# One plain pair of feed-forward units instead of two, with VectorE's order of sums written out by hand

## The chip, the cores and the metric

The kernel runs on one core of a Trainium2 chip. The core has a matrix engine (TensorE, in the profile PE for matmuls and PEld for weight loads), a vector engine (VectorE, DVE), a scalar engine (ScalarE, ACT), GpSimd (POOL) and a queue engine that starts transfers (SyncE, SP). Each works through its own queue in order and waits on semaphores for the others. The metric is the device time of one execution in microseconds (us); smaller is better. The time before is the median of three runs.

## The reference

One layer of a hybrid decoder for two groups of requests at once, a prompt of 1024 tokens and 8 samples of 8 tokens, 1088 columns in all: windowed attention beside a convolution branch, both gated, then an output projection, a residual sum, and a feed-forward block with a short convolution. The change lies in the feed-forward block:

```python
up = rmsnorm(h, norm2_g) @ w_up                  # 1024 -> 2 x 2816
uc = dwconv_valid(up_ext, ffn_conv_w, ffn_conv_b)  # 3 taps along the tokens
gate, val = jnp.split(uc, 2, axis=-1)
y = h + (jax.nn.silu(gate) * val) @ w_down
```

All is float32. The 2816 gate columns are 22 units of 128, the value columns 22 more; gate unit f and value unit f make pair f.

## The kernel before

Activations lie transposed: 128 of the model's columns on the partitions, tokens along the free dimension. A float32 product is made of three matmuls in a faster type: each operand is split into a high part (a cast on ScalarE) and a low part (the difference, on VectorE), and `mm3` (L190) adds high x high, high x low and low x high. `split_ps` (L226) makes such a pair of parts and remembers the cast in `self.cast` and the difference in `self.low`. `w_load` and `w_split` load and split whole weight units.

The 1088 columns are four quarters of 272. `norm2` (L1292) makes the normalised rows of one quarter, splits them into `hh` and `hl`, and also writes them to memory (`d_n`). The up-projection, `ffn_up` (L1333), then runs over the 22 pairs in two ways.

- A **plain** pair (`plain`, L1432) multiplies two weight units with all four quarters over all eight blocks of 128 rows. Pairs 0 and 1 are plain (`PLAIN = 2`). In pair 0 the two units take turns by quarter; in pair 1 one unit follows the other.
- A **product** pair (`pair`, L1522) treats the two units, the two halves of the columns and the two halves of the rows as a 2 x 2 block product and makes it with seven half-size products instead of eight. The rows enter as blocks "11", "21" and "22", which are parts that the norm has made, and as four sums T1 to T4. The weights enter as four blocks and three sums, made on VectorE (`plan_pair`, L1488) and split into a ring of four tiles; `prep(n)` makes sure that n of them are traced. Seven products run in an order `seq`; each adds to bank A, E or C and is followed by an eviction into the pair's `st` rows: a copy on ScalarE where the row is new, a sum on VectorE where it is not. The next product on the same bank waits for that eviction.

The sums T1 to T4 serve all product pairs and are made once. `words(n)` (L1455) loads one of four groups of rows back from memory, four transfers on SP's queue, and `sums()` (L1467) makes of each group four differences on VectorE and splits each (16 differences, 16 casts, 16 low parts in all). Groups 0 and 1 need quarters 0 and 2, groups 2 and 3 need quarters 1 and 3.

After a pair, `finish` (L1402) makes the three-tap convolutions of its two units (one tap on ScalarE, two on VectorE, 1104 columns each), the gate and the store.

What sets the order: instructions are traced in the program's order, each with a priority that counts up; a planner puts them on each engine's queue by priority among those that it takes to be ready. `later(n)` shifts the priority of a block by n, and `issue_after(x)` puts what a block traces on x's engine behind x in that engine's queue. Tiles of one tag share `bufs` places and a new one waits for the release of an old one; in `ffn_up`'s pool, places lie in the order in which the tags are first used, over memory that the output projection has used before.

Of the kernel before, what the change touches and what calls it, by code (L numbers as in the profile page):

```python
# [9 lines left out]
ALU = mybir.AluOpType  # L10
AX = mybir.AxisListType

P = 128
# [23 lines left out]
AW = FW - 2  # L37
QW = T // 4
QUARTERS = [(c * QW, QW) for c in range(4)]
PLAIN = 2  # L40
PLAIN_LATER = 240
AHEAD = 3
UP_LATER = 100
# [11 lines left out]
HALF = T // 2  # L55
# [67 lines left out]
class Build:  # L123
# [1209 lines left out]
    def ffn_up(self, hh, hl, mp):  # L1333
        nc, tc, a, pool = self.nc, self.tc, self.a, self.pool
        f_es, t_es = ExitStack(), ExitStack()
        ft = pool(f_es, "ft")
# [9 lines left out]
        first = n_up + 2 * PLAIN  # L1346
# [10 lines left out]
        def slot(i):  # L1357
            if i < n_up:
                return old_slot(i)
            if i < first:  # L1360
                return (ft, ("wraw2", "wraw2")) if i == first - 1 else (self.wp, (i - first) % 2)
            if i == n_dn:
                return self.wp, 0
            if i == n_dn + 2:
                return self.wp, 1
            if i == n_dn + 3:
                return None, [self.t(self.ds, [P, T], f"e{x}", F32R)[:, :DM] for x in (7, 8)]
            if i in places:
                return None, [self.t(mp, [P, T], f"m{y}{places[i]}", F32R)[:, :DM] for y in "hl"]
            return self.wp, i % 2  # L1370
# [61 lines left out]
        def plain(f):  # L1432
            fs = (f, NF + f)
            ws = [self.weight(("up", x), 2 - n if f == 0 else 1) for n, x in enumerate(fs)] if f == 0 else [None] * 2
            both = [up_start(x) for x in fs]
            if f == 0:
                for c in range(4):
                    for w, b in zip(ws, both):
                        self.stream(None, xs, b[3], chunks=(c,), w=w, table=QUARTERS)
            else:  # L1440
                for x, b in zip(fs, both):
                    self.stream(("up", x), xs, b[3], chunks=range(4), table=QUARTERS)
            if f == 0:
                with self.later(-60):
                    sums()
            finish(f, both, PLAIN_LATER)

        def g_raws(n):
            for f in self.groups[n]:
# [4 lines left out]

        def words(n):  # L1455
            j, kk = groups[n]
            if n % 2:
                r = [self.t(ft, [P, FW], "acc", bufs=3)[:, :4 * QW].rearrange("p (x a b) -> p x a b", x=2, a=2)
                     for _ in range(2)]
                r = [t[:, x] for t in r for x in range(2)]  # L1460
            else:
                r = [self.t(ft, [P, 2, QW], "s", bufs=4) for _ in range(4)]
            for t, c, y in zip(r, (j, 2 + j, 2 + j, j), (0, 0, 1, 1)):
                nc.sync.dma_start(t, self.d_n[c, y][:, kk:kk + 2])
            loaded[n] = r

        def sums():  # L1467
            sub = lambda o, x, y: nc.vector.tensor_tensor(o, x, y, ALU.subtract)
            for n, (j, kk) in enumerate(groups):
                r11, r12, r22, r21 = loaded[n]  # L1470
                sub(r11, r12, r11)
                sub(r12, r22, r12)
                sub(r22, r22, r11)
                sub(r21, r21, r22)
                for x, r in enumerate((r11, r22, r12, r21)):
                    self.split_ps(th[x][j][:, kk:kk + 2], tl[x][j][:, kk:kk + 2], r)
                if n + 2 < len(groups):
                    words(n + 2)

        ring = {"n": 0, "tiles": []}  # L1480
        T1, T2, T3, T4 = range(4)
        B = {"11": lambda j: (hh[j][0], hl[j][0]), "21": lambda j: (hh[j][1], hl[j][1]),
# [3 lines left out]
        preps = []  # L1486

        def plan_pair(f):  # L1488
            i = n_up + 2 * f
            hw = DM // 2  # L1490
            live = {}

            def raws():
                while len(self.w_raw) < min(i + 4, len(self.order)):
                    self.w_load()
                ra, rb = self.w_raw[i:i + 2]
                live.update(a11=ra[:, :hw], a12=ra[:, hw:], a21=rb[:, :hw], a22=rb[:, hw:])
# [12 lines left out]

            preps.extend([
                split("a11"),
                split("a21", ("a11", "a11", "a21", ALU.subtract), ("a21", "a21", "a22", ALU.add)),
                split("a21", ("a21", "a22", "a11", ALU.subtract)),
                split("a21", ("a21", "a12", "a21", ALU.subtract)),
                split("a11"), split("a12"), split("a22")])

        def prep(n):
            while ring["n"] < min(n, len(preps)):
                preps[ring["n"]]()  # L1520

        def pair(f):  # L1522
            base = 7 * (f - PLAIN)
# [5 lines left out]
                ("A", "11", True, pg, 0, copy), ("E", T1, True, pv, 2, copy), ("A", T2, False, pg, 2, copy),  # L1529
                ("E", "22", False, pg, 2, plus), ("A", T3, False, pv, 2, plus), ("C", "21", True, pg, 0, plus),  # L1530
                ("A", T4, False, pv, 0, copy)]
            for n, (bank, b, fresh, parts, c, op) in enumerate(seq):
                prep(base + n + 1 + AHEAD)
                if f == NF - 1 and n == 4:
                    self.w_hl += [None] * (n_dn - len(self.w_hl))
                    self.w_stop = len(self.order)
                    for _ in self.groups[0]:
                        self.w_load()
                        self.w_split()
                wh, wl = ring["tiles"][base + n]  # L1540
                for j in range(2):
                    if fresh:
                        banks[bank, j] = self.bank("mm" if bank == "A" else "aux")
                    ps = banks[bank, j]
                    xh, xl = B[b](j)
                    for k in range(KT // 2):
                        ks = slice(k * P, (k + 1) * P)
                        self.mm3(ps[:, :QW], wh[:, ks], wl[:, ks], xh[:, k, :], xl[:, k, :],
                                 fresh and k == 0, k == KT // 2 - 1, not fresh)
                    for d, r in parts(c + j):  # L1550
                        op(d, r(ps))  # L1551
            finish(f, both)

        for f in range(PLAIN, NF):
            plan_pair(f)
        words(0)
        words(1)
        for f in range(PLAIN):
            plain(f)
        self.w_used = self.order.index(("dn", 0))  # L1560
# [360 lines left out]
```

## Time and profile before

| | |
|---|---|
| median of three runs | 1650.48 us (1650.45 to 1651.6) |
| the profiled execution | 1651.15 us, span 1649.3 us |
| TensorE matmuls busy | 1640.4 us, 99% of the span |
| VectorE busy | 1373.2 us, 83% |
| ScalarE busy | 864.8 us, 52% |
| granted TensorE clock | 1.00 |

The profile is of one execution. A row of the timeline has the start in us from the span's start, the duration, the engine, the line of the kernel, the operation, the tiles out<-in with their shape, how many instructions the row stands for, and in brackets how long the engine was idle before and who released it. A row of the windows has, for a stretch of time, the busy time of each engine with its count of instructions, then the granted clock, the share of the transfer engines and GB/s. A row of waits has the waiting engine and line, the one waited for, the total in us, how often, and the longest.

### The profile page before, as it was taken

What the parts mean: (1) busy time and instruction counts of PE and PEld (TensorE: products, weight loads), DVE (VectorE), ACT (ScalarE), POOL (GpSimd) and SP (SyncE); (2) the same over time, 40 slices, a digit from 0 to 9 for tenths busy, and PEclk for the clock granted to TensorE, in tenths of its full rate; (3) what the DMA queues carried; (4) which work ended last, traced back from release to release, by engine and by line L of the source; (5) the groups of instructions that cost most, each with busy time, mean ns of one, the idle gap of its engine ahead of it and who ended that gap; (6) DMA issues with size and microseconds to landing.
All of it is one profiled execution on the core that took longest, in us unless ns stands there. A gap on an engine that the chain in (4) does not pass through costs nothing. (4 is left out here: it accounts for less than half of the span.)

```text
span 1649.3 us, 30197 instructions
## 1 busy us (share of the span) xinstructions
PE 1640.4 (99%) x11606; PEld 1624.3 (98%) x11606; DVE 1373.2 (83%) x2474; ACT 864.8 (52%) x1795; POOL 257.3 (16%) x549
## 2 busy tenths in 40 slices
PE   9999999999999999999999999999999999999998
PEld 9999999999999999999999999999999999999997
DVE  7899979999979996788755887888888787989867
ACT  6524277774488845575533454444444454524222
POOL 0100112222011111121003421222222110000000
PEclk9999999999999999999999999999999999999999
DMA  6221222323121255648763532343334334766423
GB/s 210 84 63 51 63 73 69 100 92 99 55 62 41 90 191 188 197 149 217 200 217 107 188 107 79 107 115 113 114 114 117 92 100 135 262 158 165 109 61 109
DMA packets 104281, 200.47 MB, mean 122 GB/s; under 512 B 25928, under 2 KB 56648, under 8 KB 104120
## 3 DMA queue, kind: packets, MB, share of 16 engines
q1 hardware_dynamic: 80952, 130.49, 25.7%
q0 software_dynamic: 22752, 67.79, 14.0%
q8 instruction: 91, 1.49, 0.4%
q14 instruction: 54, 0.44, 0.1%
q10 hardware_dynamic: 432, 0.27, 0.1%
HBM read 136.44 MB, written 64.03 MB: 122 GB/s over the span
## 5 line engine op out<-in xcount | busy, mean ns | idle before, releaser
L192 PE MATMUL mm<-xh,whi 128*128 128x384 f32 (+1 forms) x904 | 301.5, 333 | 0.0
L194 PE MATMUL mm<-xh,wlo 128*128 128x384 f32 (+1 forms) x904 | 295.4, 327 | 0.0
L193 PE MATMUL mm<-xl,whi 128*128 128x384 f32 (+1 forms) x904 | 295.3, 327 | 0.1
L193 PEld LDWEIGHTS mm<-xl,whi 128*128 128x128 f32 x904 | 170.1, 188 | 1.2 <-DVE xl L279 0.4
L192 PEld LDWEIGHTS mm<-xh,whi 128*128 128x128 f32 x904 | 170.0, 188 | 0.7
L194 PEld LDWEIGHTS mm<-xh,wlo 128*128 128x128 f32 x904 | 169.7, 188 | 0.1
L1399 DVE SCALAR_TENSOR_TENSOR acc<-st,fc,acc 128x1104 f32<-128x1104 f32 x88 | 120.1, 1365 | 3.2 <-ACT acc L1397 1.9
L173 ACT CAST whi<-wraw 128x1024 fp32r<-128x1024 f32 (+1 forms) x65 | 62.7, 970 | 74.2 <-PE mm L193 53.1
L227 ACT CAST whi<-wraw 128x512 fp32r<-128x512 f32 x84 | 52.6, 626 | 76.8 <-PE aux L194 34.9
L227 ACT CAST wlo<-wraw 128x512 fp32r<-128x512 f32 x84 | 52.6, 626 | 74.9 <-PE aux L194 43.2
L522 DVE SCALAR_TENSOR_TENSOR bt<-u,consts,bt 128x513 f32<-128x513 f32 x120 | 89.7, 748 | 0.7
L522 DVE SCALAR_TENSOR_TENSOR c<-sm,hsum,c 128x512 f32<-128x512 f32 x120 | 89.6, 746 | 0.7
L192 PE MATMUL mm<-mh,whi 128*128 128x272 f32 (+4 forms) x296 | 88.1, 298 | 0.0
L194 PE MATMUL mm<-mh,wlo 128*128 128x272 f32 (+4 forms) x296 | 87.8, 297 | 0.0
L522 DVE SCALAR_TENSOR_TENSOR c<-u,consts,c 128x512 f32<-128x512 f32 x112 | 83.7, 747 | 0.5
L228 DVE TENSOR_TENSOR wlo<-wraw,wlo 128x512 fp32r<-128x512 f32 x84 | 60.9, 725 | 27.3 <-ACT wlo L227 25.5
L193 PE MATMUL mm<-ml,whi 128*128 128x272 f32 (+4 forms) x280 | 82.9, 296 | 0.0
L228 DVE TENSOR_TENSOR whi<-wraw,whi 128x512 fp32r<-128x512 f32 x84 | 57.9, 689 | 26.9 <-ACT whi L227 25.3
L174 DVE TENSOR_TENSOR wlo<-wraw,whi 128x1024 fp32r<-128x1024 f32 (+1 forms) x65 | 72.7, 1122 | 8.5 <-ACT whi L173 7.2
L1551 ACT COPY st<-mm 128x272 f32<-128x272 f32 (+2 forms) x140 | 46.9, 350 | 50.4 <-PE mm L194 50.4
L192 PE MATMUL aux<-mh,whi 128*128 128x272 f32 (+4 forms) x232 | 69.7, 300 | 0.0
L193 PE MATMUL mm<-tl,wlo 128*128 128x272 f32 x240 | 69.6, 290 | 0.0
(650 smaller groups left out, 5735.4 us busy)
## 6 DMA issues: line engine op xcount, KB each, us to landing
wraw<-wall SPq DMA_DIRECT2D x118, 512.0 KB, 4.4
bw<-d_b SPq DMA_DIRECT2D x42, 272.0 KB, 4.0
d_b<-gd POOLq DMA_DIRECT2D x36, 272.0 KB, 7.2
d_b<-acc POOLq DMA_DIRECT2D x24, 272.0 KB, 4.0
ar<-wdn SPq DMA_DIRECT2D x32, 192.0 KB, 3.4
d_g<-acc POOLq DMA_DIRECT2D x10, 544.0 KB, 4.2
ga<-d_ga SPq DMA_DIRECT2D x8, 544.0 KB, 4.5
ct<-d_c SPq DMA_DIRECT2D x8, 544.0 KB, 6.0
```

What stands on the lines that cost most here:

```text
L173: self.cast = self.nc.scalar.copy(h[:, z], r[:, z]).ins
L174: self.nc.vector.tensor_tensor(l[:, z], r[:, z], h[:, z].bitcast(F32), ALU.subtract)
L192: mm(ps, wh, xh, start=first, stop=False, skip_group_check=more)
L193: mm(ps, wh, xl, start=False, stop=False, skip_group_check=more)
L194: self.last_mm = mm(ps, wl, xh, start=False, stop=last, skip_group_check=more).ins
L227: self.cast = self.nc.scalar.copy(h, src).ins
L228: self.low = self.nc.vector.tensor_tensor(l, src, h.bitcast(F32), ALU.subtract).ins
L522: mac = lambda o, x, w: nc.vector.scalar_tensor_tensor(o, x, w, o, ALU.mult, ALU.add)
L1399: nc.vector.scalar_tensor_tensor(acc, st[:, k:k + AW], fw(f, k), acc, ALU.mult, ALU.add)
L1551: op(d, r(ps))
```

## The change

The constant `PLAIN` goes from 2 to 1, so pair 1 becomes a product pair. In that pair alone the product with block "21" comes second, right behind "11" (both need no sum), ahead of T1. The weight blocks are prepared in the same order.

`sums()` now chains all its steps with `issue_after`: each difference, each split and each weight part of pair 1 is put behind the step before it on VectorE's and on ScalarE's queue. Per group the order is difference, split (T1), difference, difference, split (T2), difference; the splits for T3 and T4 come at once in the first group and at the end for the other three. Between them stand the weight parts of pair 1: `prep(2)` after group 0, `prep(4)` after group 2, `prep(5)` after group 3, `prep(6)` and `prep(7)` among the last splits. The convolutions of plain pair 0 are put behind the chain's end, and so are pair 1's evictions, but for that of "11", which is put behind the first split's cast (`self.mark`).

The words of group 2 go to other buffers (two of tag `gd`, one of `acc`), so that they needn't wait for group 0's. The raw weights of pair 1 are loaded ahead of plain pair 0. The split weights of pair 0's second unit go into the two `wraw2` buffers, the first unit's into `whi1` and `wlo1`; two of the first down weights get other places.

```diff
-PLAIN = 2
+PLAIN = 1
@@ slot
-                return (ft, ("wraw2", "wraw2")) if i == first - 1 else (self.wp, (i - first) % 2)
+                return (ft, ("wraw2", "wraw2")) if i == first - 1 else (self.wp, 1)
             if i == n_dn:
-                return self.wp, 0
+                return self.wp, ("wlo1", "whi0")
             if i == n_dn + 2:
-                return self.wp, 1
+                return self.wp, ("wlo0", "whi1")
@@ plain
-            finish(f, both, PLAIN_LATER)
+            with tc.issue_after(self.chain[0]), tc.issue_after(self.chain[1]):
+                finish(f, both, PLAIN_LATER)
@@ words
-            if n % 2:
+            if n in (1, 2):
                 r = [self.t(ft, [P, FW], "acc", bufs=3)[:, :4 * QW].rearrange("p (x a b) -> p x a b", x=2, a=2)
-                     for _ in range(2)]
+                     for _ in range(3 - n)]
                 r = [t[:, x] for t in r for x in range(2)]
-            else:
+            if n == 2:
+                d = [self.t(ft, [P, HALF], "gd", bufs=2).rearrange("p (a b) -> p a b", a=2) for _ in range(2)]
+                r = [d[0], r[0], d[1], r[1]]
+            if n in (0, 3):
                 r = [self.t(ft, [P, 2, QW], "s", bufs=4) for _ in range(4)]
@@ sums
-            sub = lambda o, x, y: nc.vector.tensor_tensor(o, x, y, ALU.subtract)
-            for n, (j, kk) in enumerate(groups):
+            late = []
+
+            def step(go):
+                with ExitStack() as es:
+                    for x in self.chain:
+                        es.enter_context(tc.issue_after(x))
+                    self.chain = [go() or self.low, self.cast]
+
+            def sub(o, x, y):
+                step(lambda: nc.vector.tensor_tensor(o, x, y, ALU.subtract).ins)
+
+            def parts(n, x, r):
+                j, kk = groups[n]
+                step(lambda: self.split_ps(th[x][j][:, kk:kk + 2], tl[x][j][:, kk:kk + 2], r))
+
+            for n in range(len(groups)):
                 r11, r12, r22, r21 = loaded[n]
                 sub(r11, r12, r11)
+                parts(n, 0, r11)
+                self.mark = self.cast
                 sub(r12, r22, r12)
                 sub(r22, r22, r11)
+                parts(n, 1, r22)
                 sub(r21, r21, r22)
-                for x, r in enumerate((r11, r22, r12, r21)):
-                    self.split_ps(th[x][j][:, kk:kk + 2], tl[x][j][:, kk:kk + 2], r)
-                if n + 2 < len(groups):
-                    words(n + 2)
-
+                late += [(n, 2, r12), (n, 3, r21)]
+                if n == 0:
+                    words(2)
+                    while late:
+                        parts(*late.pop(0))
+                    words(3)
+                for x in ((1, 2), (), (3, 4), ())[n]:
+                    step(lambda: prep(x))
+            step(lambda: prep(5))
+            for part in sorted(late, key=lambda v: v[1]):
+                parts(*part)
+                if part[:2] == (3, 2):
+                    step(lambda: prep(6))
+            step(lambda: prep(7))
+
+        self.chain = []
@@ plan_pair
+            if f == PLAIN:
+                go.insert(1, go.pop(5))
+            preps.extend(go)
@@ pair
+            if f == PLAIN:
+                seq.insert(1, seq.pop(5))
             for n, (bank, b, fresh, parts, c, op) in enumerate(seq):
-                prep(base + n + 1 + AHEAD)
+                with ExitStack() as es:
+                    for x in self.chain if f == PLAIN else ():
+                        es.enter_context(tc.issue_after(x))
+                    prep(base + n + 1 + AHEAD)
...
-                    for d, r in parts(c + j):
-                        op(d, r(ps))
+                    with ExitStack() as es:
+                        for x in ([self.mark] if n == 0 else self.chain) if f == PLAIN else ():
+                            es.enter_context(tc.issue_after(x))
+                        for d, r in parts(c + j):
+                            op(d, r(ps))
@@ ffn_up
         words(0)
         words(1)
+        while len(self.w_raw) < first + 2:
+            self.w_load()
```

More of the change, by code (lines that the diff above doesn't have):

```diff
@@ L1509, in split @@
                 return go
-            preps.extend([
+            go = [
                 split("a11"),
@@ L1515, in plan_pair @@
                 split("a21", ("a21", "a12", "a21", ALU.subtract)),
-                split("a11"), split("a12"), split("a22")])
+                split("a11"), split("a12"), split("a22")]
+            if f == PLAIN:
+                go.insert(1, go.pop(5))
+            preps.extend(go)
         def prep(n):
```

## The prediction

> **What bounds the kernel now.** I read the page first, then who waited for whom on TensorE, then busy time by stage around the up-projection's start, then VectorE, ScalarE and the DMA queue in order of time there.
>
> ```profile
> span 1649.3 us, 30197 instructions
> PE 1640.4 (99%) x11606; PEld 1624.3 (98%) x11606; DVE 1373.2 (83%) x2474; ACT 864.8 (52%) x1795; POOL 257.3 (16%) x549
> ```
>
> ```profile
> PE mm L653 <- DVE warm L646: 1.1, 1, 1.1
> PE aux L420 <- ACT pth L227: 0.8, 1, 0.8
> ```
>
> TensorE is the bound of the whole; its waits (the two longest are shown) are under 3 us in all, none of them here. So a matmul removed is time saved and a TensorE wait added is time lost, each one for one. The question is who feeds TensorE where a stage is removed.
>
> ```profile
> core 0: us, PE busy (x) PEld busy (x) DVE busy (x) ACT busy (x) POOL busy (x), PEclk, DMA share, GB/s
> 921.50:946.20 24.70, 24.70 (x196) 24.62 (x195) 19.54 (x35) 12.05 (x27) 7.30 (x21) 1.00 0.62 202
> 946.20:958.30 12.10, 12.10 (x98) 12.10 (x97) 12.10 (x19) 7.49 (x14) 1.47 (x3) 1.00 0.45 157
> 958.30:970.40 12.10, 12.10 (x98) 12.10 (x97) 12.10 (x17) 8.61 (x14) 5.36 (x6) 1.00 0.01 1
> ```
>
> ```profile
> 921.55 0.29 PE L192 MATMUL mm<-mh,whi 128*128 128x272 f32 x1
> 958.32 0.29 PE L192 MATMUL mm<-mh,wraw 128*128 128x272 f32 x1
> 970.43 0.29 PE L192 MATMUL mm<-mh,whi 128*128 128x272 f32 x1
> ```
>
> Plain pair 0 starts at 921.55; the two units of plain pair 1 run from 946.2 (12.1 us before the change of weight tile at 958.32) to 970.43, where the first product pair starts. In just the 24.2 us of plain pair 1 VectorE is busy all the time: it makes there the operand sums that the products read. That is the cover which the change takes away.
>
> **The matmuls.** A plain unit is 4 quarters x 8 blocks x 3 = 96 matmuls in 970.43 - 958.32 = 12.11 us, 0.126 us each. A plain pair is 192, a product pair 7 x 2 x 4 x 3 = 168. One pair changes kind: 24 x 0.126 = 3.03 us saved, 0.18% of the time, the most that the change can give. The product pair now starts at 946.2 and would end at 967.4 where plain pair 1 ended at 970.43.
>
> **The chain on VectorE.** These rows give its prices.
>
> ```profile
> 933.36 0.45 DVE L228 TENSOR_TENSOR ml<-111l,mh 128x272 fp32r<-128x272 f32 x1 [0.45 <-ACT mh L227]
> 934.60 1.23 DVE L174 TENSOR_TENSOR wraw<-wraw,wraw 128x1024 fp32r<-128x1024 f32 x1 [0.79 <-ACT wraw L173]
> 935.74 1.48 DVE L1468 TENSOR_TENSOR s<-s,s 128x544 f32<-128x544 f32 x2
> 938.30 0.73 DVE L228 TENSOR_TENSOR tl<-s,th 128x544 fp32r<-128x544 f32 x1 [1.08 <-ACT th L227]
> ...
> 950.00 0.71 DVE L1468 TENSOR_TENSOR acc<-acc 128x544 f32<-128x544 f32 x1
> 950.63 0.71 DVE L1468 TENSOR_TENSOR s<-s,s 128x544 f32<-128x544 f32 x1
> ...
> 952.55 0.71 DVE L1468 TENSOR_TENSOR s<-s,s 128x544 f32<-128x544 f32 x1
> ...
> 960.23 0.69 DVE L228 TENSOR_TENSOR whi<-wraw,whi 128x512 fp32r<-128x512 f32 x1
> 960.84 1.36 DVE L1399 SCALAR_TENSOR_TENSOR acc<-st,fc,acc 128x1104 f32<-128x1104 f32 x1
> ...
> 962.11 0.72 DVE L228 TENSOR_TENSOR tl<-acc,th 128x544 fp32r<-128x544 f32 x1
> ```
>
> ```profile
> 937.62 1.20 ACT L227 CAST th<-s 128x544 fp32r<-128x544 f32 x2
> ...
> 953.29 0.65 ACT L227 CAST th<-s 128x544 fp32r<-128x544 f32 x1 [0.34 <-DVE s L1468]
> ...
> 958.39 0.62 ACT L227 CAST whi<-wraw 128x512 fp32r<-128x512 f32 x1 [0.64 <-PE mm L193]
> 958.92 0.64 ACT L227 CAST th<-acc 128x544 fp32r<-128x544 f32 x1
> ```
>
> A sum of 544 columns takes VectorE 0.635 us from start to start (950.00 to 950.63), a low part the same, a weight instruction of 512 columns 0.61 (960.23 to 960.84). A low part needs ScalarE's cast first: the sum of 952.55 ends at 953.26, the cast starts 0.03 later and takes 0.65, and a low part follows a cast by 0.03 (first cast of 937.62 over at 938.27, low part at 938.30). So a low part right behind the sum that it splits starts 0.71 + 0.03 + 0.65 + 0.03 = 1.42 us after that sum's start, not 0.635: VectorE stands for 0.79 us. In the weights it is 0.69 + 0.03 + 0.62 + 0.03 - 0.61 = 0.76.
>
> Before, the order was free, and other sums stood between most sums and their low parts. Now `step` pins VectorE and ScalarE each to one order: per group sum, part, sum, sum, part, sum. Both of these parts stand right behind their own sum (a group's other two follow later: the first group's at once, the rest at the chain's end). Nothing else may fill the hole, since the evictions and the convolutions of plain pair 0 are pinned behind the whole chain.
>
> Start: the last low part of the second norm is at 933.36, so VectorE is free at 933.7. Work on the second plain unit's weights (below) moves this by some 0.3: 934.0. The first group's words are no limit:
>
> ```profile
> 896.91 25.01 SPq L1464 DMA_DIRECT2D s<-d_n  x4
> DMA to landing us min/median/max: 2.8/3.3/4.9
> ```
>
> The four transfers are issued by 921.9 and land by 921.9 + 4.9 = 926.8. Yet the weight split of 934.60, which is traced later and so ranks lower, went ahead of the first sum at 935.74: the planner took the words to be ready only after the norm, and I expect no sum among the norm's instructions.
>
> Up to the sum for the weights of product "22" (`prep(5)`) the chain holds 26 instructions of 544 columns (8, 6, 6, 6) and 7 of 512 (two parts, then five for `prep(3)` and `prep(4)`): 26 x 0.635 + 7 x 0.61 = 20.8 us. Standing: 8 x 0.79 + 2 x 0.76 = 7.8. So the sum of `prep(5)` starts at 934.0 + 28.6 = 962.6. From there only ScalarE counts, for all its casts are pinned: 0.72 to the first one, then three weight casts (0.53 from start to start, 958.39 to 958.92) and six of 544 columns (0.55, from two in 1.20) up to the end of `prep(7)`'s: 0.72 + 3 x 0.53 + 6 x 0.55 = 5.6, so 968.2.
>
> The eviction of T1's product is a ScalarE copy pinned behind that last cast. The same bank takes product "22" next, so TensorE waits for it: one copy, here 0.39 + 0.03, to 968.6.
>
> ```profile
> 937.33 0.39 ACT L1390 COPY st<-mm 128x272 f32<-128x272 f32 x1 [2.48 <-PE mm L194]
> ```
>
> Then "22", T3 and T4 run without a wait, 3 x 24 x 0.126 = 9.1: the pair ends at 977.7. The low parts come in time (`prep(5)`'s at 962.6 + 1.37, then two weight parts and six others behind it, so that the last is over by 969.7; T4 starts at 974.7). Copies of plain pair 0 on ScalarE, one or two each 3 us until 949, can make a cast late: between 0 and 8 x 0.39 = 3.1 us; most fall into ScalarE's idle time, I take 0.5. End 978.2 against 970.43: +7.8.
>
> The wait is not one gap. T1 has its weights (`prep(3)`) only at about 955 instead of 952.3, its second half waits for the fourth group until 959.5, and T2 is done by 964; the last gap, to 968.6, is the longest, 4.6 us.
>
> **The second plain unit's weights** now go into two `wraw2` buffers which, by the order of first use in the pool, come to lie on the last output unit's weights.
>
> ```profile
> 921.42 0.29 PE L194 MATMUL mm<-t,t 128*128 128x272 f32 x1
> 933.50 1.07 ACT L173 CAST wraw<-wraw 128x1024 fp32r<-128x1024 f32 x1
> ```
>
> These are read until 921.71; cast 1.07 and low part 1.23 end at 924.0, and the second unit starts 24 matmuls and the norm's mean after 921.55, at 924.8. Cost on TensorE nothing by that order, some 0.3 on the norm. If the split ran where the split into `wraw2` ran before (933.5), plain pair 0 would be 10 us late, but the pair's end, set by the chain, would hardly move. That is why I charge 0 here.
>
> **What costs nothing.** The third and fourth groups' words: their rows are written with the norm's last parts (933.8 at the latest), two landings of 4.9 make 943.6, and the third group's first sum is at 947.5. The two early weight loads stand on SP's queue ahead of them, waiting for the split at 924.0, when no word is ready to be loaded. Plain pair 0's convolutions (4 x 1.27, then the gate) go from under plain pair 1 to behind 969.6; the next pair's first eviction needs their buffers at 981, five us after they can be done. POOL's store of plain pair 0's result goes with them; it is read only near the stage's end. The eviction of "11" stays early by `mark`. At the stage's end, the last pair's raw weights now share two buffers with the first down weights:
>
> ```profile
> 1382.50 0.69 DVE L228 TENSOR_TENSOR wlo<-wraw,wlo 128x512 fp32r<-128x512 f32 x1 [1.40 <-ACT wlo L227]
> ...
> 1384.51 1.05 ACT L173 CAST whi<-wraw 128x1024 fp32r<-128x1024 f32 x1 [2.05 <-PE aux L194]
> ```
>
> The pair's last weight part is over by 1383.2; a load as slow as the words' slowest (4.9), a cast and a part (2.3) end at 1390.4. At 1384.5 a product that frees the cast's buffer has ended, and three are still to run, 9.1 us, until 1393.6; only then are the down weights read. No cost.
>
> **Sum.** -3.03 for the matmuls, +10.8 of waits (978.2 - 967.4): +7.8. On the profiled execution, 1651.15 us (span 1649.3 and 1.85 around it), 1658.9; it is 0.67 above the median of 1650.48, which gives **1658.3**, 0.5% slower. About 0.2%, 3.3 us, is what a measurement of this kernel can tell from no change.
>
> **The clock.** Every window above has a granted clock of 1.00, beside TensorE pauses of 1.1 us at most. A pause of 4.6 us is new to this kernel.
>
> ```profile
> 1.05 5.49 PE L653 MATMUL mm<-mean 128*128 128x128 f32 x24 [1.05 <-DVE warm L646]
> ```
>
> The first 24 matmuls of the program, after idleness, took 0.23 us each for 128 columns, where 272 columns now take 0.126: TensorE can be slow after a pause. By the rows the price is between 0 and one product at half pace, 24 x 0.126 = 3.0; I take 0, as no pause in mid-kernel shows it. [...]
>
> **The rivals.**
> 1. The chain begins among the norm's instructions (words are there at 926.8, VectorE is nearly full until 933.7). Then the first two groups' holes, 4 x 0.79 = 3.2, are filled. From 926.8: the norm's rest (933.7 - 926.8 = 6.9) + 20.8 + 7.8 - 3.2 = 32.3, `prep(5)`'s sum at 959.1, the pair's end 3.5 earlier: +4.3, 1654.8. Against it: the order at 934.60.
> 2. The cover holds and the saving arrives: 1647.5. This is the other side. It needs "22" not to wait, so `prep(5)`'s sum by about 952.2, which is 10.4 us earlier than I put it; even with no hole at all the work of 20.8 from 933.7 ends at 954.5. It could be only if the order on VectorE were not serial as I read `step`.
> 3. The clock drops in the last gap: one product at half pace, +3.0, 1661.3.
> 4. Worse backlog: the convolutions, 4 x 1.27 + 1.2 + 0.2 = 6.5 us, stand ahead of the next pair's weights and TensorE waits for them too: up to 1664.8.
>
> **Chances.** The forecast 0.52 (its own range 1655.3 to 1660.9: the 0.5 between 0 and 3.1, the start up to 2.5 earlier); rival 1 0.15; rival 2 0.06; rival 3 0.19; rival 4 0.08. The range goes from 1652.0, below rival 1, to 1664.0. Slower by over 0.2% (above 1653.8): 0.52 + 0.19 + 0.08 and some 0.06 of rival 1, which may fill more holes than I count, 0.85; within 0.2%: the rest of rival 1 and most of rival 2, 0.13; faster 0.02, as the largest saving is itself below the bound.
>
> **What would show it.** In the profile after: 24 matmuls fewer; TensorE waits on VectorE's low parts or ScalarE's casts between 952 and 969, at T1, then at "22" behind the copy of T1's bank; VectorE's idle time before low parts 0.8 each, "<-ACT th"; a first sum at 934. I am wrong if the first sum starts by 930, if low parts don't wait for casts, or if T1's copy stands ahead of the last casts.

## The result, and the profile after

The changed kernel takes 1664.56 us (median of five runs, 1664.29 to 1666.61), the kernel before 1650.45 beside it: a ratio of 1.0088, with a 95% interval of 1.0073 to 1.0102, 14.1 us more. The prediction had 1658.3, 7.8 more, in a range that ended at 1664.0, 0.6 below the result. The direction was right and the size was not.

The page of the changed kernel, its first two lines:

```profile
span 1662.5 us, 30166 instructions
PE 1640.5 (99%) x11582; PEld 1623.3 (98%) x11582; DVE 1380.3 (83%) x2491; ACT 866.6 (52%) x1800; POOL 257.0 (15%) x549
```

There are 24 matmuls fewer, yet TensorE's busy time is what it was (1640.4): some of those that are left are slower. TensorE's longest waits there (waiting line, releaser, total, times, longest), and the stage in windows from the start of plain pair 0:

```profile
PE aux L192 <- ACT whi L227: 7.1, 1, 7.1
PE aux L192 <- ACT st L1594: 5.7, 1, 5.7
```

```profile
core 0: us, PE busy (x) PEld busy (x) DVE busy (x) ACT busy (x) POOL busy (x), PEclk, DMA share, GB/s
921.20:945.88 24.68, 24.68 (x197) 24.60 (x195) 16.30 (x31) 10.20 (x25) 7.02 (x21) 1.00 0.70 220
945.88:951.93 6.05, 6.05 (x50) 5.99 (x48) 4.59 (x8) 1.74 (x4) 0.38 (x2) 1.00 0.63 219
951.93:959.16 7.23, 0.16 (x2) 0.00 (x1) 5.01 (x9) 1.91 (x3) 0.00 (x0) 0.80 0.00 0
959.16:967.63 8.47, 8.44 (x48) 7.99 (x48) 6.29 (x10) 2.48 (x5) 0.00 (x0) 0.77 0.00 0
967.63:973.45 5.82, 0.17 (x3) 0.01 (x1) 5.08 (x9) 5.28 (x11) 0.00 (x0) 0.70 0.06 8
973.45:978.03 4.58, 4.58 (x24) 4.58 (x25) 4.55 (x8) 3.84 (x8) 0.00 (x0) 0.64 0.67 219
978.03:984.20 6.17, 6.17 (x51) 6.17 (x50) 6.12 (x12) 5.02 (x6) 4.54 (x6) 1.00 0.01 4
```

Plain pair 0, then "11" and "21", run as before. Then TensorE waits 7.23 us for T1's weights, takes 8.47 us for T1 and T2 (6.05 at full pace), waits 5.82 for the copies of T1's bank, and takes 4.58 for "22" (3.02 at full pace). The clock of 1.00 that every window before showed is 0.64 to 0.80 here. The pair ends at 984.20, 38.32 us after its start where 24.2 (the plain pair) minus 3.03 was ideal: 17.1 of waits and slow matmuls, less 3.03, is the 14.1.

VectorE and ScalarE in order of time there:

```profile
933.63 0.72 DVE L1481 TENSOR_TENSOR s<-s,s 128x544 f32<-128x544 f32 x1
937.96 0.73 DVE L228 TENSOR_TENSOR tl<-s,th 128x544 fp32r<-128x544 f32 x1 [3.62 <-ACT th L227]
938.61 1.48 DVE L1481 TENSOR_TENSOR s<-s,s 128x544 f32<-128x544 f32 x2
940.99 0.72 DVE L228 TENSOR_TENSOR tl<-s,th 128x544 fp32r<-128x544 f32 x1 [0.90 <-ACT th L227]
...
945.92 0.72 DVE L1481 TENSOR_TENSOR acc<-acc 128x544 f32<-128x544 f32 x1
947.36 0.72 DVE L228 TENSOR_TENSOR tl<-acc,th 128x544 fp32r<-128x544 f32 x1 [0.71 <-ACT th L227]
...
967.40 0.69 DVE L1536 TENSOR_TENSOR wraw<-wraw,wraw 128x512 f32<-128x512 f32 x1
968.82 0.69 DVE L228 TENSOR_TENSOR whi<-wraw,whi 128x512 fp32r<-128x512 f32 x1 [0.74 <-ACT whi L227]
```

```profile
937.00 0.39 ACT L1390 COPY st<-mm 128x272 f32<-128x272 f32 x1 [2.64 <-PE mm L194]
937.28 0.65 ACT L227 CAST th<-s 128x544 fp32r<-128x544 f32 x1
940.02 0.39 ACT L1390 COPY st<-mm 128x272 f32<-128x272 f32 x1 [2.09 <-PE mm L194]
940.31 1.20 ACT L227 CAST th<-s 128x544 fp32r<-128x544 f32 x2
943.05 0.45 ACT L1390 COPY st<-mm 128x208 f32<-128x208 f32 x2 [1.55 <-PE mm L194]
...
962.61 0.65 ACT L227 CAST th<-s 128x544 fp32r<-128x544 f32 x1 [1.40 <-DVE s L1481]
963.16 0.67 ACT L1594 COPY st<-mm 128x272 f32<-128x272 f32 x2
...
972.50 0.61 ACT L227 CAST whi<-wraw 128x512 fp32r<-128x512 f32 x1
973.01 0.72 ACT L1594 COPY st<-aux 128x272 f32<-128x272 f32 x3
```

The first sum runs at 933.63, as forecast. But its cast stands on ScalarE behind a copy of plain pair 0 that waits until 937.00 for TensorE, and so do the next casts: the second group begins at 945.92, not at the 941.9 that the prediction's prices give (934.0 + 8 x 0.635 + 2 x 0.79 + 2 x 0.61). From there on each low part that stands right behind its own sum has 0.7 us of idleness ahead of it.

Two things that the section on the change says, and the prediction with it, are not so in the trace. The eviction of "11" isn't behind the first split's cast: `self.mark` is set again in each group, and the rows of 962.61 and 963.16 show the copies behind the last group's. TensorE shows no wait there. And plain pair 0's weights don't go into new places: both units are split before `ffn_up` begins, during the output projection, into `whi` and `wlo`, and the trace has no other split of a whole unit up to 1000 us:

```profile
850.73 1.05 ACT L173 CAST whi<-wraw 128x1024 fp32r<-128x1024 f32 x1 [2.92 <-DMA wraw<-wall]
858.83 1.05 ACT L173 CAST whi<-wraw 128x1024 fp32r<-128x1024 f32 x1 [2.04 <-PE mm L193]
```

By the order in the program the first unit lies in `whi0` and `wlo0`, which are the places of pair 1's first two weight parts; e2 shows what that costs.

### The profile page after: what moved, and what is told of

It reads as the page before. It is cut to its first block, busy times and chain, and to the rows that moved or that the text cites. A ratio compares the mean times of both kernels' runs of the same rounds, so it can differ in the third digit from the quotient of the medians.

```text
span 1662.5 us, 30166 instructions
## 1 busy us (share of the span) xinstructions
PE 1640.5 (99%) x11582; PEld 1623.3 (98%) x11582; DVE 1380.3 (83%) x2491; ACT 866.6 (52%) x1800; POOL 257.0 (15%) x549
## 5 line engine op out<-in xcount | busy, mean ns | idle before, releaser
L228 DVE TENSOR_TENSOR whi<-wraw,whi 128x512 fp32r<-128x512 f32 x88 | 63.7, 724 | 30.1 <-ACT whi L227 28.5
L174 DVE TENSOR_TENSOR wlo<-wraw,whi 128x1024 fp32r<-128x1024 f32 (+1 forms) x62 | 69.0, 1118 | 7.1 <-ACT whi L173 6.8
L193 PE MATMUL mm<-tl,wlo 128*128 128x272 f32 x256 | 74.3, 290 | 0.0
L194 PE MATMUL mm<-th,wlo 128*128 128x272 f32 x256 | 74.0, 289 | 0.0
L192 PE MATMUL mm<-th,wlo 128*128 128x272 f32 x256 | 73.8, 288 | 0.0
L192 PE MATMUL mm<-mh,whi 128*128 128x272 f32 (+4 forms) x248 | 73.1, 295 | 0.0
L193 PE MATMUL mm<-tl,whi 128*128 128x272 f32 x248 | 71.9, 290 | 0.0
```

The costliest lines, as they stand in the source:

```text
L174: self.nc.vector.tensor_tensor(l[:, z], r[:, z], h[:, z].bitcast(F32), ALU.subtract)
L192: mm(ps, wh, xh, start=first, stop=False, skip_group_check=more)
L193: mm(ps, wh, xl, start=False, stop=False, skip_group_check=more)
L194: self.last_mm = mm(ps, wl, xh, start=False, stop=last, skip_group_check=more).ins
L228: self.low = self.nc.vector.tensor_tensor(l, src, h.bitcast(F32), ALU.subtract).ins
```

## The experiments

Three theories went in. A: the end of pair 1 is set by the pinned queues, and each of their delays has its own price: the holes on VectorE (its idle time between a sum and the low part that stands right behind it), copies ahead of casts on ScalarE, the evictions behind the chain's end. B: the slow clock after the pauses is what the prediction lacked. C: VectorE has too much work here once the plain pair is gone, in whatever order. The first four runs added D: VectorE's backlog, so that a wait taken from pair 1 comes back in pair 2.

Most runs write the queues of the stage out as lists, each instruction with `issue_after` behind the one ahead of it. In the lists, S is a difference, P a part (on ScalarE its cast, on VectorE its low part) of group a to d for T1 to T4, A a weight sum and W a weight part; c2 and c3 are the copies of plain pair 0's third and fourth quarter (g, v); 11, T1, ... are pair 1's evictions; a tap is one of the three terms of plain pair 0's convolutions, and conv one of those on VectorE. Written out in the changed kernel's order the lists give its stage: in e10, which only adds matmuls to it, T1 and "22" start 37.97 and 52.28 us after plain pair 0, in the changed kernel 37.96 and 52.24.

The table has each run's median, its distance from the kernel before beside it, and from the rows of its trace the start of T1, of "22", and the end of pair 2 (the first matmul of pair 3), counted from the start of plain pair 0. The medians are good to about 1 us; the last column shows smaller differences within the stage.

| run | us | minus before | T1 | "22" | pair 2 done |
|---|---|---|---|---|---|
| before | 1650.45 | 0 | | | 70.04 |
| changed | 1664.56 | +14.1 | 37.96 | 52.24 | 84.03 |
| e1 evictions placed | 1664.20 | +13.0 | 37.96 | 47.92 | 83.17 |
| e2 casts first | 1664.04 | +12.8 | 36.83 | 51.11 | 84.20 |
| e3 no holes, casts first | 1651.43 | +0.2 | 30.74 | 39.53 | 69.87 |
| e4 all three | 1651.62 | +0.4 | 30.73 | 36.84 | 70.44 |
| e5 unpinned | 1651.86 | +0.9 | 32.71 | 40.07 | 70.97 |
| e6 next weights first | 1648.17 | -2.8 | 30.73 | 36.78 | 67.85 |
| e7 kept busy | 1666.49 | +15.5 | 37.98 | 52.26 | 85.18 |
| e8 before, pinned | 1651.35 | +0.3 | | | 70.41 |
| e9 holes only | 1654.28 | +3.1 | 30.87 | 42.02 | 73.80 |
| e10 kept busy, pinned | 1664.21 | +13.0 | 37.97 | 52.28 | 82.62 |
| e11 e1 without taps | 1661.80 | +10.6 | 37.96 | 47.92 | 81.36 |
| e12 next casts first | 1647.78 | -3.4 | 30.73 | 36.78 | 67.11 |
| e13 start freed | 1661.23 | +10.0 | 34.00 | 48.28 | 80.48 |
| e14 holes back | 1656.12 | +4.9 | 34.00 | 43.69 | 75.51 |

### e1: the evictions placed

```diff
 ScalarE
-W5 Pb3 Pc3 Pd3 W6 Pb4 Pc4 Pd4 W7 T1a T1b T2a T2b
+W5 T1a T1b Pb3 Pc3 Pd3 W6 T2a T2b Pb4 Pc4 Pd4 W7
```

> Both queues of the stage are written out as one list, in the order that the changed kernel has, with one edit: the copies of T1's product stand on ScalarE right behind the cast of the weights for block 22, and T2's right behind the next weight cast, not behind the chain's last cast. Theory A (the pair's end is ScalarE's chain, with the evictions queued behind its end): by hand, with the durations of the changed kernel's trace, the 5.7 us wait before 22 shrinks to under 1 us, but 1.8 us come back before T4, so the pair ends 2.0 us earlier, and another 1.6 us if TensorE then isn't slow in 22: 1661.0 to 1662.6. Theory B (the slow clock after the pauses is what the prediction lacked): the pause of 7 us before T1 stays and so does its slow stretch; only 22 runs at full pace, 1.6 us less, 1663.0. Theory C (VectorE has too much work and its order doesn't matter): 1664.5.

"22" starts 4.3 us earlier, but pair 2 is done only 0.9 earlier. The pause before "22" is 1.3 us now and "22" runs at nearly full pace: the three groups of 24 matmuls that hold its own have means of 301, 288 and 288 ns, in the changed kernel 325, 315 and 312. The gain goes to new waits, at T4 for VectorE's sum (1.2 us) and in pair 2 for its weights (1.3, 0.9 and 0.2). Theory A had a wait before T4 in its sum; no theory had those in pair 2.

### e2: the casts first

```diff
 ScalarE
-c2g Pa1 c2v Pa2 Pa3 c3g Pa4 W1 W2 c3v Pb1 Pb2
+Pa1 c2g Pa2 Pa3 Pa4 c2v W1 W2 Pb1 c3g Pb2 c3v
```

> One edit to the changed kernel's order: the copies of plain pair 0's third and fourth quarter stand on ScalarE behind the casts that are ready before them (the first behind the chain's first cast, not ahead of it). VectorE's order and the pinned evictions stay. Theory A (a copy that waits for TensorE holds up the cast behind it, and with it VectorE): first low part at 935.1 and not 938.0, the group 3.6 us earlier, the chain's end too; pair 1 ends 3.6 us earlier, 1661.0, and if the shorter wait before T1 (3.5 us) brings no slow stretch, up to 1.6 us less, 1659.4. Theory B (slow clock): both pauses are still there (3.5 and 4.7 us), so 1664. Theory C (amount of VectorE's work): 1664.5.

T1 is 1.1 us earlier, not 3.6. The copies hold nothing up any more, but the first weight part does. ScalarE and VectorE of this run:

```profile
942.60 0.62 ACT L1508 CAST whi<-wraw 128x512 fp32r<-128x512 f32 x1 [2.51 <-PE mm L202]
```

```profile
943.25 0.69 DVE L1495 TENSOR_TENSOR whi<-wraw,whi 128x512 fp32r<-128x512 f32 x1 [2.81 <-ACT whi L1508]
```

Its place is free only when the matmuls of the first plain unit's last quarter end. The profile before has the same wait, at plain pair 1's first unit:

```profile
943.26 1.05 ACT L173 CAST whi<-wraw 128x1024 fp32r<-128x1024 f32 x1 [1.42 <-PE mm L193]
```

Behind the copies this wait was covered; without them it is the next in line. The clock then took the rest of the gain: it was 0.5 for 10.24 us from 967.97 here, and "22" took 5.6 us.

### e3 and e4: no holes, and all three

```diff
 VectorE (e3 and e4; e4 also has 21a 21b ahead of Sd4)
-Sa1 Pa1 Sa2 Sa3 Pa2 Sa4 Pa3 Pa4 W1 W2 Sb1 Pb1 Sb2 Sb3 Pb2 Sb4 Sc1 Pc1 Sc2 Sc3 Pc2 Sc4 A3 W3 A4 W4 Sd1 Pd1 Sd2 Sd3 Pd2 Sd4 A5 W5
+Sa1 Sb1 Sa2 Pa1 Sb2 Pb1 Sa3 Sb3 Sa4 Pa2 Pb2 Pa3 Pa4 W1 W2 Sc1 Sc2 Sb4 Pc1 A3 Sc3 W3 A4 Sd1 Pc2 W4 Sd2 Pd1 Sd3 A5 Sc4 Pd2 W5 Sd4
 ScalarE (e4; e3 has the copies of T1 and T2 behind W7)
+... Pd3 T1a W6 T1b Pb4 Pc4 Pd4 T2a W7 T2b
```

> As the run with the casts first, and VectorE's order is changed too: another group's sum or weight sum stands between a sum and the low part made of it, so that VectorE never waits for a cast; the evictions stay behind the chain's last cast. Theory A: the last weight part of the four that 22 needs moves from 968 to 954.5, the last cast to 958, and TensorE waits 0.4 us in the pair, 967.8 at its end (before: 970.4): 1647.8, below both kernels. Theory B has nothing to slow the clock when the waits are gone, the same 1648. Theory C: the 33 instructions that 22 waits for are still 20.8 us of VectorE after 933.7, with 2 us of low parts and copies behind: no better than 1655.

> All three edits in one order: casts first, no holes, and the copies of T1 and T2 and the sums of block 21 at the place where they are ready. Theory A: no wait of TensorE in the pair, the full 3.03 us of the matmuls saved: 1647.4; as the run before it has 0.4 us of waits left, the two differ by 0.4 us at most. If the difference is larger, placing the evictions is worth more than my schedule by hand has it. Theory C: no better than 1655.

Both come out at the kernel before's time (ratios 1.0001, intervals 0.9992 to 1.0010 and 0.9993 to 1.0010), 13 us under the changed kernel: theory C is out, and the clock is 1.00 in e4's windows below and in e3's in the last section. But neither is below before, which A had. TensorE's waits of e3 and of e4:

```profile
PE aux L201 <- ACT st L1516: 2.6, 1, 2.6
```

```profile
PE aux L201 <- ACT whi L236: 1.3, 2, 0.9
PE aux L203 <- DVE whi L237: 0.6, 1, 0.6
PE mm L201 <- ACT wlo L236: 0.2, 1, 0.2
```

e3 waits at "22" for its pinned copy, e4 doesn't, and waits 2.1 us in pair 2 instead, at its T1, T2 and "22", for weights. Two windows of e4, pair 1 and pair 2, show why:

```profile
945.79:967.27 21.48, 21.48 (x171) 21.27 (x170) 21.26 (x38) 15.12 (x30) 2.34 (x6) 1.00 0.25 81
967.27:991.55 24.28, 22.17 (x171) 21.29 (x169) 23.17 (x35) 13.11 (x24) 11.23 (x14) 1.00 0.25 85
```

VectorE is busy nearly all the time (21.26 of 21.48, then 23.17 of 24.28): the sums, then plain pair 0's convolutions, then pair 2's weights. That is theory D.

### e5: the changed kernel without its pins

```diff
 step() in sums()
-    for x in self.chain:
-        es.enter_context(tc.issue_after(x))
-    self.chain = [go() or self.low, self.cast]
+    go()
 and the same for the pins of evictions, weights and finish()
```

> The changed kernel without any of its pins: the sums, splits, weight parts, evictions and convolutions stand as the planner puts them, and all else (one plain pair, 11 and 21 first, the buffers) stays. Theory A (the pinned order is what costs): the planner puts other work between sums and their low parts and the evictions where their products end; with its queues laid out by hand TensorE waits 2.8 us before T1 and 1.0 in T2, so the pair ends at 971.3 where the changed kernel's ends at 984.6: 1651.3, up to 1652.6 with a convolution's tap on ScalarE between casts. Theory D, from the runs so far (VectorE's work until pair 2 is a bound; a wait taken from pair 1 comes back in pair 2): about 1651 as well, with waits in pair 2. Theory C (one plain pair less costs 14 us in any order): 1664.

1651.86, 0.9 above before, which is no difference that the runs can tell (ratio 1.0004, 0.9995 to 1.0013). One plain pair less costs nearly nothing in the planner's own order, where a wait of 1.8 us before T1 and one slow stretch behind it (3.41 us at a clock of 0.50) take back what the matmuls save; the pinned order costs the rest.

### e6 and e12: the next pair's weights ahead of the convolutions

```diff
 VectorE
+... Pa4 Sc1 Sc2 W1 W2 ... W7 22a 22b W8 A9 T3a T3b W9 A10 conv W10 conv conv conv
 ScalarE, e6 and e12
+... Pa4 c2v Pc1 W1 W2 ... T2a W7 T2b W8 tap tap W9 (e6: T4a T4b W10, e12: W10 T4a T4b)
```

> The run with all three edits, and the work behind the chain written out too: the first three weight blocks of pair 2 stand ahead of the convolutions of plain pair 0, ScalarE's Silu behind these casts; and in the chain the first two sums of the third group stand ahead of pair 1's first weight parts, which wait for plain pair 0's matmuls until 943.2. Theory A with a backlog behind it (pair 2's four waits of 2.7 us, for weights that stand behind convolutions, are all that is left): no wait in pair 1 nor in pair 2, 2.7 us under the run with all three, that is 2.5 below before. Theory D (VectorE simply has too much work here): the wait turns up in pair 2's block 22 or T3, or in its evictions, whose st buffers are free only after the convolutions, and the time stays within 0.5 us of before.

> The fastest run so far with one edit: the cast of pair 2's third weight block stands ahead of the two copies of T4, which wait for TensorE until 969.5 and kept VectorE idle for 1.75 us. Theory D (VectorE's free time is what counts in pair 2): the 0.85 us that TensorE still waits in pair 2 shrink by 0.5 or more, 0.4 to 0.8 below that run, that is 3.0 to 3.6 us below before. Rival: its last waits come from evictions on ScalarE, and it is the same within 0.3 us.

e6 is 2.8 us under before (0.9979, 0.9970 to 0.9988), e12 3.4 (0.9982, 0.9973 to 0.9991): both are faster than both kernels, and than the one before by about the 3.03 of the matmuls. The step from e6 to e12 is within the medians' spread, but in the last column it is 0.74, as expected. e12's windows of plain pair 0, pair 1 and pair 2:

```profile
921.74:946.44 24.70, 24.70 (x197) 24.62 (x196) 21.45 (x40) 12.08 (x28) 9.38 (x21) 1.00 0.79 245
946.44:967.50 21.06, 21.06 (x170) 21.06 (x169) 20.84 (x38) 13.98 (x28) 2.35 (x6) 1.00 0.26 85
967.50:988.85 21.35, 21.35 (x170) 21.29 (x170) 20.18 (x29) 12.65 (x23) 5.81 (x11) 1.00 0.21 77
```

TensorE has no wait, VectorE is busy 62.47 of the 67.11 us (21.45 + 20.84 + 20.18). Theory D's backlog is real, but it fits.

### e7 and e10: TensorE kept busy

```diff
+for _ in range(n):   # e7: 50 before T1, 40 before "22"; e10: 55, 24 before T1's second half, 36, each pinned in TensorE's queue
+    nc.tensor.matmul(idle[:, :QW], self.identr, hh[0][0][:, 0, :], start=True, stop=True)
```

> The changed kernel with added work: 50 matmuls of 272 columns into an unused bank before T1 (6.3 us at 0.126, in its wait of 7.1) and 40 before 22 (5.0 us, in the wait of 5.7), so that TensorE isn't idle in its two waits. Their results are not used. Theory B (the slow clock after a pause): no slow stretch; T1 and T2 take 6.1 us and not 8.5, which the chain takes back as a longer wait before 22, and 22 takes 3.0 and not 4.6: 1.55 us less, 1663.0. Rival: the slow stretches cost nothing, because ScalarE's chain sets the end whatever TensorE does: 1664.5 or, as the added matmuls stand in TensorE's queue, up to 0.5 more.

> The changed kernel's two orders written out, TensorE's too, with added matmuls of 272 columns pinned into its three waits: 55 before T1, 24 before T1's second half, 36 before 22 (6.9, 3.0 and 4.5 us); their results are not used. The run before with added matmuls left a pause of 3.5 us before 22, and 22 ran wholly in a slow stretch. Theory B, the clock's share: no stretch below full clock in this stage, 22 takes 3.0 us and not the changed kernel's 4.6, and starts at the same place, since ScalarE's chain sets it: 1.5 us below the changed kernel, 1663.0, and 3.5 below the run before. Rival: the time of the changed kernel, as something else than the pause slows 22.

In e7 the planner moved some of the added matmuls up, which left a pause of 3.5 us before "22", and "22" took 5.6 us at a clock of 0.50: 1.4 worse than the changed kernel. T1 and T2 ran at full pace (clock 1.00 from 953.4 to 969.1), and "22" started where it had (52.26 us, in the changed kernel 52.24). So the slow clock in T1 and T2 costs nothing here; the chain sets the start of "22". In e10, "22" has a window at full clock:

```profile
974.78:977.92 3.14, 3.14 (x25) 3.14 (x25) 3.01 (x7) 3.14 (x8) 0.00 (x0) 1.00 0.64 222
```

Pair 2 is done 1.41 us earlier than in the changed kernel. That is the clock's share of the 14.1.

### e8: the kernel before with its sums pinned

```diff
 before.py, sums(): each sub() and split_ps() in a step()
+with issue_after(last low or sum), issue_after(last cast): ...
```

> The kernel before, with both plain pairs, and of the change only the order of the sums: each difference and split pinned behind the step before, in the changed kernel's order (difference, split, difference, difference, split, difference; the splits for T3 and T4 at once in the first two groups, at the end in the others). Weights, evictions and convolutions are free. Theory A (the plain pair is a cover of 24.2 us): the chain, 32 x 0.635 + 8 x 0.79 = 26.6 us of VectorE from 934, with two taps and five weight instructions among it, ends about 966 to 970, T1 reads from 973.4: no change, within 0.5 us of before. If the pinned order were bad in itself, TensorE would wait at T1 or T2 of the first product pair, and the time be 2 to 6 us longer.

No change (ratio 1.0004, 0.9995 to 1.0013). With the plain pair as a cover of 24 us the same pinned order of the sums is free.

### e9: the holes alone

```diff
 VectorE as in e3; ScalarE keeps the copies ahead of the casts, evictions behind W7
+c2g Pa1 c2v Pb1 Pa2 Pb2 Pa3 c3g Pa4 W1 W2 c3v Pc1 W3 Pc2 W4 Pd1 ...
```

> The changed kernel with one edit, VectorE's order without holes (the order of the run with no holes); plain pair 0's copies stand ahead of the chain's first casts as in the changed kernel, and the evictions behind the chain's last cast. Theory A (the holes are the largest price): by hand the pair ends 9.8 us earlier, with no slow stretch 1.6 more: 1653.2; what VectorE's backlog takes back in pair 2 comes on top, 0 to 2 us. Rival (the copies and the place of the first weight block set the chain's start, the holes come second): the start of the second group stays where it is, about 945 against 945.9, and the gain is under 5 us, 1660 or more.

+3.1 and a last column 10.2 below the changed kernel's: one edit takes back three quarters of the loss, which puts the rival out. Part of it may be that VectorE, with other sums to do, isn't held up by the late casts; this run doesn't part the two. A pause of 3.1 us before "22" is left, and "22" still takes 4.58.

### e11: e1 without plain pair 0's taps on VectorE

```diff
-for k in (1, 2):
+for k in (1, 2) if f % NF else ():
```

> The run with the evictions placed, with plain pair 0's four convolution taps on VectorE left out (4 x 1.28 us; pair 0's result is not the reference's). Theory D (the 4.3 us that placing the evictions gained at block 22 went to VectorE's backlog in pair 2: its weights stand behind the convolutions): pair 2's waits at T1, T2 and 22, 2.9 us, are gone and the time is 2.5 to 3 us below the run with the taps, 1661. Rival (the waits in pair 2 come from ScalarE or from the evictions' buffers): no more than 1 us below it.

Pair 2 is done 1.8 us earlier than in e1, and the time is 2.3 under e1's distance from before: a little under the 2.5 that was expected at least. Pair 2 keeps waits of 0.4 and 0.3 us for weights, which this run doesn't explain.

### e13 and e14: the start freed, and the holes put back

```diff
 VectorE, both runs
-W1 W2 Sb1 Pb1 Sb2
+Sb1 Pb1 Sb2 W1 W2
 ScalarE, both runs; e13 is e2 with this edit, e14 is e12 with the changed kernel's order of sums and parts
-c2v W1 W2 Pb1 c3g Pb2 c3v
+c2v Pb1 W1 W2 c3g Pb2 c3v
```

> The run with the casts first, and pair 1's first two weight parts stand behind the first part and the second sum of the second group, so that their wait for plain pair 0's matmuls (until 943.1) holds up nothing. Holes and evictions stay as in the changed kernel. If the copies and the place of the first weight block together are what made the chain late: the second group's first sum starts at 940.7 and not 944.5 or 945.9, T1 at 20 us less than the changed kernel's end of the chain by hand, that is 3.6 us ahead of the changed kernel's, and 22 3.6 us ahead too; 1661.0, or 1659.4 to 1662.3 by what the clock does after the pauses. Rival (the first group's words or ScalarE's own pace make it late): the second group at 944 or later and 1663 or more.

> The fastest version with the holes put back: VectorE's order in the chain is the changed kernel's (a part right behind its own sum), the first two weight parts a little later as in the run beside this one; casts first, evictions where they are ready, and the next pair's weights first, as in the fastest version. By hand pair 1 ends at 975.1 where the fastest version's ends at 967.4: 7.7 us, which is the prediction's 7.8 for the holes; 1655.5, and up to 1.5 more if a pause of 3.5 us before T1 brings a slow stretch that isn't hidden. Rival (VectorE's backlog is the bound, holes or not, so that part of the holes is filled by work that would otherwise stand in pair 2): under 5 us above the fastest version, 1653 or less.

e13's second group starts at 941.13, 19.5 us after plain pair 0's start (changed kernel 24.7); T1 and "22" are 3.96 earlier, pair 2 done 3.55 earlier, as "22" takes 4.99 us in a slow stretch and not 4.58.

```profile
941.13 0.72 DVE L1523 TENSOR_TENSOR acc<-acc 128x544 f32<-128x544 f32 x1
```

The late start of the chain is those two things, the copies and the first weight block's place. With the copies alone out of the way the weight block holds the chain (e2); the weight block alone out of the way was not run.

From the changed kernel to e13, e14 and e12 the last column goes 84.03, 80.48, 75.51, 67.11. So: 3.55 us for the start; 4.97 for the evictions and the next weights in their places, with "22" at 3.60 us in e14, where it waits for its own weights (4.99 in e13); 8.40 for the holes, which e14's rows show at 0.68 to 0.78 us each. The sum, 16.9, stands against the 17.1 of waits and slow matmuls. In another order the steps would share the sum otherwise: the holes alone were worth 10.2 (e9).

## Why the prediction was right in direction and short in size

- **The matmuls, -3.03.** Right: 11606 to 11582, and e12 gets 2.93 of it within the stage.
- **The chain's start, 934.0.** Right: 933.63. Rival 1 (a start among the norm) is out.
- **The holes, 7.8.** Right: 0.68 to 0.75 each behind the first group, where 0.76 and 0.79 were taken, and 8.40 when put back (e14).
- **"Copies of plain pair 0 on ScalarE can make a cast late: between 0 and 8 x 0.39 = 3.1 us; I take 0.5."** This is the step that failed. It priced a copy by its own 0.39 us. A copy in ScalarE's queue also waits for its matmuls (2.64, 2.09 and 1.55 us in the rows above), and the casts behind it wait with it: the second group came 4.0 late. The row from which the 0.39 was taken, 937.33, has such a wait in its brackets, 2.48 us. The bound of 3.1 from above was wrong as well. A second wait stands behind this one and has no term in the prediction: the place of pair 1's first weight part is the first plain unit's until that unit's last matmuls end (942.6 in e2). Freeing the copies alone moves "22" by 1.1 us and the end of pair 2 not at all (e2); freeing both moves "22" by 3.96 and the end by 3.55 (e13). ScalarE kept its queue's order here: a cast ready at 934.4 starts at 937.28, behind the copy of 937.00.
- **The sum of `prep(5)` at 962.6.** 967.40: the 4.0, and 0.8 more in the chain, part of it that a sum which overwrites what the sum right before it reads starts 0.75 us after it and not 0.635 (two in 1.48).
- **ScalarE's tail of 5.6, then one copy.** Right: 967.40 to the last cast's end at 973.11, and "22" at 973.45. The wait of 4.6 forecast there is 5.8, that before T1 7.2 where 3 was forecast.
- **The clock, taken at 0 with a rival of 3.0.** The rival's half pace was an estimate: the row it points at, 24 matmuls of 0.23 us, ran at a granted clock of 1.00 (the first 6.5 us of the trace before). The changed kernel then had 0.50 from 969.92 to 976.75. So this is a term that was mis-sized: 1.55 us in "22" (4.58 against 3.03), 1.4 when undone in e10. Forecast and rival 3 were held apart, and the case came as both. 978.2 + 4.3 (start and chain, 4.8 less the 0.5 taken) + 1.6 (clock) makes 984.1; 984.20 was measured.
- **Backlog, rival 4.** Not in the changed kernel, whose late chain leaves pair 2 free of waits for weights. It is what takes the gain back as soon as the chain is faster (e1, e4).
- **The second plain unit's weights.** The charge of 0 came out, by luck: the split that the prediction moves to 924.0 isn't there, as both units were split by 861.2. The first unit's place is what pair 1's first weight part waits for.
- **The next words, the down weights at the end.** Right: no wait of TensorE there.
- **The cover as the reason.** Half right. e8 shows that under the plain pair the pinned order is free. But e5 shows that without it a free order comes out within 1 us of before; the loss is the pinned order's, not the missing pair's.

## What to carry to other kernels

Before pinning an order, lay out each engine's queue in order of time, with what each instruction waits for: an instruction costs those behind it its wait as well as its duration (here a copy of 0.39 us with 2.64 of wait), and the wait behind the one that you remove is the next price. Put other work between a sum and the part that needs a cast on another engine, at 0.7 us a hole here. A wait that goes from one stage is only gained when the next stage's feeder isn't late for the same reason (in e1, 4.3 us at "22" left 0.9 at the end of pair 2): go by where the next two stages end, not by the wait.

## What the runs showed of the hardware that was not expected

The clock was 0.50 for 3.41 us in e5 (from 955.11), for 6.83 in the changed kernel (from 969.92) and for 10.24 in e2 (from 967.97), one, two and three times 3.41; and the 3.41 us ahead of it had matmuls each time (1.59, 1.25 and 1.75 us). Windows of e5 and then of e3, each 3.41 us long and in step with the changes of the clock in its trace:

```profile
951.70:955.11 3.41, 1.59 (x13) 1.35 (x11) 3.41 (x7) 2.49 (x5) 0.00 (x0) 1.00 0.00 0
955.11:958.52 3.41, 3.15 (x15) 2.89 (x14) 3.41 (x6) 2.15 (x3) 0.00 (x0) 0.50 0.00 0
958.52:961.94 3.42, 3.42 (x29) 3.41 (x28) 2.66 (x5) 2.88 (x8) 0.00 (x0) 1.00 0.00 0
```

```profile
956.71:960.12 3.41, 1.68 (x14) 1.45 (x12) 3.41 (x7) 3.41 (x8) 0.00 (x0) 1.00 0.00 0
960.12:963.54 3.42, 2.57 (x20) 2.57 (x21) 3.42 (x7) 3.42 (x10) 0.00 (x0) 1.00 0.43 146
```

In e5 TensorE was idle for 1.8 us, busy 1.59 of the window's 3.41, and the next window was at 0.50, though TensorE was busy for 3.15 of it. In e3 a pause of 2.6 us, split over two windows, left 1.68 in the first, and the next was at 1.00. As e2's window of 1.75 was followed by a slow one, the matmuls in a window don't tell by themselves, in these runs, whether the next is slow. What a pause of 2 us can cost is an estimate from e5 and e3: nothing, or up to 1.7 us, half of one window of 3.41 at 0.50.
